# Gate products between the two value halves, the merge's scaled operand transposed first, and a token mix moved into two low-rank factors

## The chip, the cores and the metric

The kernel runs on one core of a Trainium2 chip. A core has five engines with queues of their own: PE (matrix products), DVE (vector), ACT (scalar and activations), POOL (a slower vector engine) and SP (which here only issues loads). Each engine works off its instructions in the order that was fixed when the program was built; engines wait for each other through semaphores. The metric is the device time of one execution in microseconds, the median of several runs.

## What is computed

A block of two models in one program, for 256 tokens of width 1024, all in float32. The part that the change touches is the first layer, an RWKV-7 time mix, of which these lines matter:

```python
h_prev = jnp.pad(h, ((0, 0), (1, 0), (0, 0)))[:, :-1]
hh = h_prev - h
xr = h + hh * mu[0]; xw = h + hh * mu[1]; xk = h + hh * mu[2]
xv = h + hh * mu[3]; xa = h + hh * mu[4]; xg = h + hh * mu[5]
r = xr @ w_r
w = -jax.nn.softplus(-(w0 + jnp.tanh(xw @ w1) @ w2)) - 0.5
k = xk @ w_k
v = xv @ w_v
a = jax.nn.sigmoid(a0 + (xa @ a1) @ a2)
g = jax.nn.sigmoid(xg @ g1) @ g2
...
def step(state, inp):
    r_t, w_t, k_t, v_t, a_t, b_t = inp
    sa = jnp.einsum('bhvk,bhk->bhv', state, a_t)
    state = state * w_t[:, :, None, :] + sa[..., None] * b_t[:, :, None, :] + v_t[..., None] * k_t[:, :, None, :]
    y_t = jnp.einsum('bhvk,bhk->bhv', state, r_t)
    return state, y_t
```

The scan over tokens is computed in four chunks of 64 tokens. In each chunk a triangular system per head has to be inverted (16 heads x 4 chunks). After this layer come a feed-forward block, a differential attention, another feed-forward block, a second token mixer and a third feed-forward block, which the change does not touch.

## The kernel before

The program is written tile by tile; a list scheduler (`schedule_with_timeline_sim=True`, L1333) then fixes the order on each engine from the dependencies, the free buffers and a timeline of its own. What comes earlier in the text goes first where several instructions are ready. `behind(m)` (L230) ties what is traced inside it behind marked instructions of the same engines.

Loads of 512 KB go through five buffers named raw (`wp("raw", 1024, NRAW)`, L263 on SP's queue, L268 on ACT's). Products of weights and activations are made of three products of a rounded part and a rest (`mm3`, L300): ACT casts the rounded part (hi), DVE or POOL subtracts the rest (lo), L273 to L277. Products of plain float32 operands stand in the trace as two records each. PSUM banks of tag p are two.

The early stage (L442 to L483): `normT` squares each token tile (ACT), adds (DVE), takes the root on POOL (L317, `power`), makes a diagonal matrix (DVE, L340) and transposes with it on PE; `ev_x` copies the result to the tiles xn (x0). `mix(j, dst)` (L445) makes one of the six token mixes: a scaled copy on ACT (L452) and a multiply-add with the tokens shifted by one on DVE (L453), 8 each for an unsplit mix. `proj_r(0)` is the first half of the r projection. Then mix 1 and mix 4 (xw, xa) are made, PE multiplies them with the two low-rank factors in wa1 (L471 to L474, 64 columns each) into lat (L475, L476: Tanh and a copy on ACT), then mix 2 (xk), `proj_r(1)`, mixes 5 and 3. Everything after xk waits in ACT's order.

A loop over four feature pairs (L549) makes k, the decays, and the matrices of the chunks (tiles G, MA, MK, RB, BT); its last PE instruction is marked `looped`.

The solve (L647 to L657): DVE transposes the small blocks (tA) and runs 30 elimination steps of two instructions. Meanwhile PE makes the values, `value_proj(n)` for the two halves n of the value width (L512, 16 products of 512 columns each, two banks), and ACT copies them to vt and, per chunk, to uvs (L667). The gate products (L671 to L678) follow in the text: 16 products in four banks of tag p, each emptied by ACT into gl. After the solve DVE makes two transposes, TX (L682) and T0 (L683), and scales T0 (L684). T0 and MA are the operands of the merge's first step (`st == 0`, L698), whose result is copied into V1 (L708); the second step (L701) uses V1 and TT, the latter copied from TX by ACT and DVE (L689). `gate_bias` (L724) multiplies vt by the bonus on DVE (L727). The chunk loop (L736) begins with the products W and then U.

Of the kernel before, what the change touches and what calls it, by code (L numbers as in the profile page):

```python
# [166 lines left out]
def body(ctx, tc, a, at):  # L167
# [26 lines left out]
    def bank(tag, pool=pt, bufs=2):  # L194
        return pool(tag, 512, bufs)
# [22 lines left out]
    def mark(*names):  # L218

        own = {getattr(mybir.EngineType, n) for n in names or ("Pool", "Activation", "DVE")}  # L220
        m = {}
        for i in reversed(nc.cur_bb.bb.instructions):
            if i.engine in own and i.engine not in m:
                m[i.engine] = i
                if len(m) == len(own):
                    break
        return m

    @contextmanager
    def behind(m):  # L230
        with ExitStack() as es:
            for i in m.values():
                es.enter_context(tc.issue_after(i))
            yield
# [4 lines left out]
    def bc(ap, shape):  # L239
        return ap.to_broadcast(shape)  # L240

    def hs(ap, d):
        return ap.rearrange("p (h d) -> p h d", d=d)
# [10 lines left out]
    def C(n):  # L254
        o, w = at[n]
        return cst[:, o:o + w]
# [10 lines left out]
    def wside(name, n=1024, rows=P):  # L267
        t_ = wp("raw", 1024, NRAW)  # L268
        nc.scalar.dma_start(t_[:rows, :n], a[name])
        return t_[:, :n]  # L270
# [26 lines left out]
    def mm(out, l, r, start=True, stop=True):  # L297
        PE.matmul(out, lhsT=l, rhs=r, start=start, stop=stop, skip_group_check=True)  # L298
# [132 lines left out]
    V.tensor_tensor(out=mab[:, 0], in0=g6, in1=mab[:, 1], op=ALU.subtract)  # L431
    xv, rT = FMt(SP, "xv"), [None] * 4
    xr, xk = pairHL(XR, "xr"), pairHL(LP, "xk")
    xw, xa, xg = FMt(EP, "xw"), FMt(EP, "xa"), FMt(XR, "xg")
    x0 = [EP("xn", 4 * (T + 1), 2).rearrange("p (k c) -> p k c", k=4) for _ in range(2)]
    for z in x0:
        G.memset(z[:, :, 0:1], 0.0)
# [7 lines left out]
    def mix(j, dst):  # L445
        for b in range(2):
            for k in (0, 2):
                k2 = slice(k, k + 2)
                d_ = dst.v[b][:, k2] if isinstance(dst, FMt) else hs(scratch("gr", 512, 2), T)
                for f in range(2):  # L450
                    ca, cb = (mab[:, i, j, 4 * b + k + f:4 * b + k + f + 1] for i in range(2))
                    S.activation(d_[:, f], x0[b][:, k + f, 1:], AF.Copy, scale=ca)  # L452
                    V.scalar_tensor_tensor(out=d_[:, f], in0=x0[b][:, k + f, :T], scalar=cb, in1=d_[:, f],  # L453
                                           op0=ALU.mult, op1=ALU.add)
                if not isinstance(dst, FMt):
                    split(d_, dst[0].v[b][:, k2], dst[1].v[b][:, k2], G if j else V)

    def proj_r(i):
        rT[i] = LP("r", 512, 4)
        S.copy(rT[i], pfm(a["w_r"], i, xr, lambda f: None if i else G))  # L460

    mix(0, xr)
    m0 = mark()
    proj_r(0)
    with behind(m0):
        mix(1, xw)
        mix(4, xa)
        m1 = mark()
    lat = LP("lat", 256)
    ps = bank("p")  # L470
    for k in range(8):  # L471
        mm(ps[0:64, :T], wa1[:, k, 0:64], xw.k(k), k == 0, k == 7)
    for k in range(8):
        mm(ps[64:128, :T], wa1[:, k, 64:128], xa.k(k), k == 0, k == 7)  # L474
    S.activation(lat[0:64], ps[0:64, :T], AF.Tanh)  # L475
    S.copy(lat[64:128], ps[64:128, :T])  # L476
    with behind(m1):
        mix(2, xk)
        m2 = mark()
    proj_r(1)  # L480
# [31 lines left out]
    def value_proj(n, acc):  # L512
        for g in range(4):
            w = hs(fetch(a["w_v"], 4 * n + g), 512)
            for k in range(2):
                kk = 2 * g + k
                for t in range(2):
                    with behind(looped):
                        mm(acc[t], xv.k(kk)[:, t * P:(t + 1) * P], w[:, k], kk == 0, kk == 7)
        for t in range(2):  # L520
            S.copy(vt[t][:, n * 512:(n + 1) * 512], acc[t])
# [135 lines left out]
        V.tensor_tensor(out=Tb[:, s + 1:, 0:s], in0=Tb[:, s + 1:, 0:s], in1=tmp[:, s + 1:, 0:s], op=ALU.add)  # L657
    solved = mark("DVE")


    for n in range(2):
        value_proj(n, [bank("v", tps) for _ in range(2)])
    for t in range(2):
        v4 = vt[t].rearrange("p (f h v) -> p f h v", f=8, h=2)
        for c in range(2):
            for hp in range(2):
                S.copy(uvs[2 * t + c][H[1 - hp], :, hp], v4[H[c], :, hp])  # L667
    gl, b1 = FMt(VP, "gl"), FMt(VP, "b1")
    g2a, g2b = wside("lora_g2"), wside("lora_g2b", 1024, 32)
    lnw, lnb = C("lnx_w"), C("lnx_b")  # L670
    for i in range(4):  # L671
        ps = bank("p")
        for f in range(2):
            fb = 2 * i + f
            fs = slice(fb * P, (fb + 1) * P)
            mm(ps[:, F[f]], g2a[:, fs], sgT[:, 0], True, False)
            mm(ps[:, F[f]], g2b[0:32, fs], sgT[0:32, 1], False, True)
        S.copy(gl.v[i // 2][:, 2 * (i % 2):2 * (i % 2) + 2], hs(ps, T))  # L678

    with behind(solved):  # L680
        T0, TX, V1 = hs(tI, 32), tmp, hs(tA, 32)
        V.transpose(TX, Tb)  # L682
        V.transpose(T0, Tb.rearrange("p t s -> p s t"))  # L683
        V.tensor_tensor(out=T0, in0=T0, in1=bc(nsb.rearrange("p f c -> p (f c)").unsqueeze(1), [P, 32, 32]),  # L684
                        op=ALU.mult)
    for qd in (1, 3, 0, 2):
# [651 lines left out]
```

## Time and profile before

| | us |
|---|---|
| median of three runs | 1212.76 (1209.64 to 1217.07) |
| the profiled execution | 1209.02 |
| its span in the trace | 1206.9 |
| PE busy | 1113.0 (92% of the span) |
| DVE busy | 858.0 (71%) |
| ACT busy | 632.5 (52%) |
| POOL busy | 194.4 (16%) |

Times in rows are microseconds from the start of the span of the profiled execution. PE is TensorE's products, PEld its weight loads, which overlap them. The span covers all stages one after another, and the change touches those between 0 and 190 us. A busy PE is not PE at its peak: the granted clock has two levels, 1.00 (2.4 GHz) and 0.50 (1.2 GHz), and the same products take twice the time at the lower one. A chain of waits is followed back from the last instruction: each piece is what released the next one.

### The profile page before, as it was taken

The numbers are of one execution on the slowest core, as the hardware profiler recorded it, in microseconds if no ns is written. First come the engines' busy times: TensorE is split into PE (matmuls) and PEld (weight loads), VectorE is DVE, ScalarE is ACT, GpSimd is POOL, SyncE is SP. The second block draws the span as 40 slices with busy tenths as digits, with TensorE's granted clock in tenths as the row PEclk, the third lists the DMA queues.
The fourth block names the chain that finished last, engine by engine and source line by source line (L and its number), as shares of the span: only waits on it lengthen the run. The fifth ranks groups of instructions, "written<-read, shape, count | busy, mean of one in ns | idle before, by whom it ended". The sixth has DMA issues, their size and how long they took to land.

```text
span 1206.9 us, 19872 instructions
## 1 busy us (share of the span) xinstructions
PE 1113.0 (92%) x7788; PEld 975.2 (81%) x7788; DVE 858.0 (71%) x1508; ACT 632.5 (52%) x1042; POOL 194.4 (16%) x156
## 2 busy tenths in 40 slices
PE   4999999779999999998999999999898789999995
PEld 4788549669999998886679999998876669999994
DVE  5687756859997566856659887554667667877787
ACT  6976145445434346757658334444867446344451
POOL 2242301200000001243130000004001112232320
PEclk8989878889999999999999999999989899999998
DMA  5354220248888563544147997662667234555551
GB/s 191 129 133 129 71 62 32 88 146 278 291 271 310 193 210 103 182 158 139 35 158 261 343 329 251 186 209 81 200 183 195 53 122 138 183 185 188 179 158 53
DMA packets 56589, 205.40 MB, mean 170 GB/s; under 512 B 6288, under 2 KB 6800, under 8 KB 56496
## 3 DMA queue, kind: packets, MB, share of 16 engines
q1 hardware_dynamic: 52128, 189.82, 47.0%
q0 software_dynamic: 2016, 7.34, 3.5%
q10 hardware_dynamic: 2352, 6.98, 1.7%
q8 instruction: 61, 1.00, 0.3%
q14 instruction: 32, 0.26, 0.1%
HBM read 203.06 MB, written 1.05 MB: 169 GB/s over the span
## 4 chain that ended last, share of the span: by engine, by line
PE 74%; DVE 12%; ACT 6%; DMA 5%; issue 2%; POOL 1%; POOLq 0%; ACTq 0%; DVEq 0%
PE p L298 31%; PE tr L298 16%; PE acc L298 14%; PE pj L298 6%; PE sc L298 3%; DVE lo L273 1%; DMA raw<-in_dn 1%; PE W L298 1%; ACT hi L276 1%; PE tr L310 1%; PE G L298 1%; PE px L298 1%; DVE cacc L1304 1%; DVE lo L655 1%; DVE lo L657 1%
## 5 line engine op out<-in xcount | busy, mean ns | idle before, releaser
L276 ACT CAST hi<-raw 128x1024 fp32r<-128x1024 f32 x198 | 205.9, 1047 | 153.9 <-PE p L298 84.1
L273 DVE TENSOR_TENSOR lo<-raw,hi 128x1024 fp32r<-128x1024 f32 x162 | 201.9, 1251 | 83.1 <-ACT hi L276 82.9
L298 PE MATMUL p<-fhh,hi 128*128 128x256 f32 x576 | 164.5, 286 | 2.5 <-ACT fhh L276 1.7
L298 PE MATMUL p<-fhl,hi 128*128 128x256 f32 x576 | 165.0, 286 | 1.2 <-DVE fhl L362 0.9
L298 PE MATMUL p<-fhh,lo 128*128 128x256 f32 x576 | 163.9, 285 | 0.0
L276 ACT CAST dhi<-raw 128x1024 fp32r<-128x1024 f32 x66 | 69.2, 1049 | 133.0 <-DMA raw<-in_dn 133.0
L298 PE MATMUL tr<-fhh,hi 128*128 128x256 f32 x480 | 136.0, 284 | 0.0
L298 PE MATMUL tr<-fhl,hi 128*128 128x256 f32 x480 | 135.9, 283 | 0.0
L298 PE MATMUL tr<-fhh,lo 128*128 128x256 f32 x480 | 135.7, 283 | 0.0
L273 DVE TENSOR_TENSOR dlo<-raw,dhi 128x1024 fp32r<-128x1024 f32 x66 | 83.6, 1267 | 56.7 <-ACT dhi L276 56.7
L273 POOL TENSOR_TENSOR lo<-raw,hi 128x1024 fp32r<-128x1024 f32 x36 | 87.8, 2441 | 189.4 <-ACT hi L276 186.0
L298 PEld LDWEIGHTS p<-fhh,hi 128*128 128x128 f32 x576 | 111.4, 193 | 4.5 <-ACT fhh L276 1.9
L298 PEld LDWEIGHTS p<-fhl,hi 128*128 128x128 f32 x576 | 111.3, 193 | 3.5 <-DVE fhl L362 1.7
L298 PEld LDWEIGHTS p<-fhh,lo 128*128 128x128 f32 x576 | 111.3, 193 | 0.3 <-issue 0.2
L298 PE MATMUL acc<-dhi,acth 128*128 128x512 f32 x264 | 103.6, 392 | 1.3 <-DVE acth L833 1.3
L298 PE MATMUL acc<-dlo,acth 128*128 128x512 f32 x264 | 103.4, 392 | 0.0
L298 PE MATMUL acc<-dhi,actl 128*128 128x512 f32 x264 | 100.7, 390 | 1.0 <-DVE actl L273 1.0
L317 POOL TENSOR_TENSOR s_rstd<-s_ms,mhalf 128x1 f32<-128x1 f32 (+2 forms) x32 | 34.8, 1091 | 361.5 <-DVE s_ms L331 272.4
L298 PEld LDWEIGHTS tr<-fhh,hi 128*128 128x128 f32 x480 | 91.9, 192 | 1.2 <-issue 0.2
L298 PEld LDWEIGHTS tr<-fhl,hi 128*128 128x128 f32 x480 | 91.9, 192 | 1.2 <-issue 0.2
L298 PEld LDWEIGHTS tr<-fhh,lo 128*128 128x128 f32 x480 | 91.9, 192 | 0.0
L888 DVE CUSTOM_DVE_ANT_0 junk<-wada,crow 128x1024 f32<-128x1024 f32 x64 | 78.0, 1219 | 8.9 <-DMA wada<-in_w_ada 7.3
(452 smaller groups left out, 2518.5 us busy)
## 6 DMA issues: line engine op xcount, KB each, us to landing
raw<-in_gu SPq DMA_DIRECT2D x132, 512.0 KB, 4.4
raw<-in_dn SPq DMA_DIRECT2D x66, 512.0 KB, 4.4
wada<-in_w_ada SPq DMA_DIRECT2D x48, 512.0 KB, 5.1
raw<-in_w_r SPq DMA_DIRECT2D x8, 512.0 KB, 4.4
raw<-in_w_k SPq DMA_DIRECT2D x8, 512.0 KB, 3.8
raw<-in_w_v SPq DMA_DIRECT2D x8, 512.0 KB, 4.7
raw<-in_w_o SPq DMA_DIRECT2D x8, 512.0 KB, 4.5
raw<-in_w_ak SPq DMA_DIRECT2D x8, 512.0 KB, 4.4
```

What stands on the lines that cost most here:

```text
L273: (eng or V).tensor_tensor(out=out, in0=raw, in1=hi.bitcast(F32), op=ALU.subtract)
L276: S.copy(hi, raw)
L298: PE.matmul(out, lhsT=l, rhs=r, start=start, stop=stop, skip_group_check=True)
L310: PE.transpose(o, s_, ident)
L317: G.tensor_tensor(out=r, in0=ms, in1=mhalf[:, :n], op=ALU.pow)
L655: V.tensor_tensor(out=tmp[:, s + 1:, 0:s], in0=bc(Ab[:, s + 1:, s:s + 1], shp), in1=bc(Tb[:, s:s + 1, 0:s], shp), op=ALU.mult)
L657: V.tensor_tensor(out=Tb[:, s + 1:, 0:s], in0=Tb[:, s + 1:, 0:s], in1=tmp[:, s + 1:, 0:s], op=ALU.add)
L888: V.tensor_tensor_reduce(out=junk, in0=raw, in1=src, scale=1.0, scalar=0.0, op0=ALU.mult, op1=ALU.add, accum_out=dst[:, e:e + 1])
L1304: V.scalar_tensor_tensor(out=a4[:, ro, co], in0=g4[:, ri, ci], scalar=taps[:, fb, k:k + 1], in1=a4[:, ro, co], op0=ALU.mult, op1=ALU.add)
```

## The change

Three edits, all in the first layer.

1. The mixes xw and xa are no longer made. Since a mix is a x_t + b x_(t-1) with a and b per feature, a and b are multiplied into the two low-rank factors instead: four products on POOL (`G.tensor_tensor`, 128 partitions x 8 x 64 each) make wmix[0] and wmix[1], each with the 64 columns of both factors. PE then multiplies wmix[0] with x0 and wmix[1] with x0 shifted by a token, 16 products of 128 columns into one bank. They stand, with Tanh and copy, ahead of mix 0 and `proj_r(0)` in the text. Mix 2 is now tied behind mix 0 instead of mix 4. The pool EP holds two tiles of wmix in place of four of xw and xa.
2. The gate products become a function that is called between `value_proj(0)` and `value_proj(1)`. The output tiles gl and b1 and the loads of the gate weights (`wside`, on ACT's queue) are now ahead of both value halves in the text, and the copies to uvs come after them.
3. T0 is transposed before TX.

```diff
--- before.py
+++ after.py
@@ -431,7 +431,13 @@
     V.tensor_tensor(out=mab[:, 0], in0=g6, in1=mab[:, 1], op=ALU.subtract)
     xv, rT = FMt(SP, "xv"), [None] * 4
     xr, xk = pairHL(XR, "xr"), pairHL(LP, "xk")
-    xw, xa, xg = FMt(EP, "xw"), FMt(EP, "xa"), FMt(XR, "xg")
+    xg = FMt(XR, "xg")
+
+    wmix = [hs(EP("wmix", 1024, 2), P) for _ in range(2)]
+    for i in range(2):
+        for j, c in ((1, slice(0, 64)), (4, slice(64, P))):
+            G.tensor_tensor(out=wmix[i][:, :, c], in0=wa1[:, :, c], in1=bc(mab[:, i, j].unsqueeze(2), [P, 8, 64]),
+                            op=ALU.mult)
     x0 = [EP("xn", 4 * (T + 1), 2).rearrange("p (k c) -> p k c", k=4) for _ in range(2)]
     for z in x0:
         G.memset(z[:, :, 0:1], 0.0)
@@ -459,22 +465,17 @@
         rT[i] = LP("r", 512, 4)
         S.copy(rT[i], pfm(a["w_r"], i, xr, lambda f: None if i else G))
 
+    lat = LP("lat", 256)
+    ps = bank("p")
+    for k in range(8):
+        for i in range(2):
+            mm(ps[:, :T], wmix[i][:, k], x0[k // 4][:, k % 4, 1 - i:1 - i + T], k + i == 0, k + i == 8)
+    S.activation(lat[0:64], ps[0:64, :T], AF.Tanh)
+    S.copy(lat[64:128], ps[64:128, :T])
     mix(0, xr)
     m0 = mark()
     proj_r(0)
     with behind(m0):
-        mix(1, xw)
-        mix(4, xa)
-        m1 = mark()
-    lat = LP("lat", 256)
-    ps = bank("p")
-    for k in range(8):
-        mm(ps[0:64, :T], wa1[:, k, 0:64], xw.k(k), k == 0, k == 7)
-    for k in range(8):
-        mm(ps[64:128, :T], wa1[:, k, 64:128], xa.k(k), k == 0, k == 7)
-    S.activation(lat[0:64], ps[0:64, :T], AF.Tanh)
-    S.copy(lat[64:128], ps[64:128, :T])
-    with behind(m1):
         mix(2, xk)
         m2 = mark()
     proj_r(1)
@@ -657,30 +658,33 @@
         V.tensor_tensor(out=Tb[:, s + 1:, 0:s], in0=Tb[:, s + 1:, 0:s], in1=tmp[:, s + 1:, 0:s], op=ALU.add)
     solved = mark("DVE")
 
-
-    for n in range(2):
-        value_proj(n, [bank("v", tps) for _ in range(2)])
+    gl, b1 = FMt(VP, "gl"), FMt(VP, "b1")
+    g2a, g2b = wside("lora_g2"), wside("lora_g2b", 1024, 32)
+    lnw, lnb = C("lnx_w"), C("lnx_b")
+
+    def gate_products():
+        for i in range(4):
+            ps = bank("p")
+            for f in range(2):
+                fb = 2 * i + f
+                fs = slice(fb * P, (fb + 1) * P)
+                mm(ps[:, F[f]], g2a[:, fs], sgT[:, 0], True, False)
+                mm(ps[:, F[f]], g2b[0:32, fs], sgT[0:32, 1], False, True)
+            S.copy(gl.v[i // 2][:, 2 * (i % 2):2 * (i % 2) + 2], hs(ps, T))
+
+
+    value_proj(0, [bank("v", tps) for _ in range(2)])
+    gate_products()
+    value_proj(1, [bank("v", tps) for _ in range(2)])
     for t in range(2):
         v4 = vt[t].rearrange("p (f h v) -> p f h v", f=8, h=2)
         for c in range(2):
             for hp in range(2):
                 S.copy(uvs[2 * t + c][H[1 - hp], :, hp], v4[H[c], :, hp])
-    gl, b1 = FMt(VP, "gl"), FMt(VP, "b1")
-    g2a, g2b = wside("lora_g2"), wside("lora_g2b", 1024, 32)
-    lnw, lnb = C("lnx_w"), C("lnx_b")
-    for i in range(4):
-        ps = bank("p")
-        for f in range(2):
-            fb = 2 * i + f
-            fs = slice(fb * P, (fb + 1) * P)
-            mm(ps[:, F[f]], g2a[:, fs], sgT[:, 0], True, False)
-            mm(ps[:, F[f]], g2b[0:32, fs], sgT[0:32, 1], False, True)
-        S.copy(gl.v[i // 2][:, 2 * (i % 2):2 * (i % 2) + 2], hs(ps, T))
-
     with behind(solved):
         T0, TX, V1 = hs(tI, 32), tmp, hs(tA, 32)
+        V.transpose(T0, Tb.rearrange("p t s -> p s t"))
         V.transpose(TX, Tb)
-        V.transpose(T0, Tb.rearrange("p t s -> p s t"))
         V.tensor_tensor(out=T0, in0=T0, in1=bc(nsb.rearrange("p f c -> p (f c)").unsqueeze(1), [P, 32, 32]),
                         op=ALU.mult)
     for qd in (1, 3, 0, 2):
```

## Rows read from the trace of the kernel before

**Rows 1.** The chain that ended last, over the whole span, in order of time: start us, length us, engine, tile and line, count.
```profile
298.75 5.75 PE p L298 x48
```

**Rows 2.** The same chain, read for 120 to 250 us (a name ahead of the tile's own, as lo or tI, is the buffer's first name).
```profile
160.58 0.11 DVE lo L657
160.72 1.25 DVE lo L682
161.96 1.83 DVE tI L683
...
166.24 1.24 DVE tI L684
...
167.61 3.00 PE mg L298 x100
170.62 4.60 PE p L298 x8
175.22 0.58 PE mg L298 x16
175.79 4.60 PE p L298 x8
180.39 3.87 PE mg L298 x140
184.26 5.68 PE W L298 x32
189.94 1.89 PE p L298 x16
```

**Rows 3.** The timeline of all engines, 132 to 168 us: start us, us from the first start to the last end, engine, line, operation, out<-in, shapes, count (of PE two records for one product of float32); in brackets the idle time before it and what ended that.
```profile
132.54 27.82 PE L298 MATMUL v<-raw,xv 128*128 128x512 f32 x64
...
160.20 4.59 PE L298 MATMUL p<-sgT,raw 128*128 128x256 f32 x16
```

**Rows 4.** Busy time of PE alone in stretches of 2 us (records begun), then its granted clock, the DMA share and GB/s.
```profile
164.00:166.00 2.00, 0.79 (x3) 1.00 0.04 14
...
168.00:170.00 2.00, 2.00 (x79) 0.50 0.03 8
...
188.00:190.00 2.00, 2.00 (x17) 0.94 0.00 0
```

**Rows 5.** The timeline of ACT, 160 to 200 us.
```profile
162.05 4.29 ACT L689 COPY TT<-lo 32x512 f32<-32x512 f32 x4 [5.35 <-DVE lo L682]
...
166.99 2.50 ACT L667 COPY uv<-vt 64x512 f32<-64x512 f32 x4
169.39 1.05 ACT L678 COPY gl<-p 128x512 f32<-128x512 f32 x2
```

**Rows 6.** The timeline of DVE, 160 to 200 us.
```profile
169.52 1.23 DVE L727 TENSOR_TENSOR vt<-vt,bonus 128x1024 f32<-128x1024 f32 x1 [2.05 <-ACT uv L667]
170.78 0.68 DVE L708 COPY tA<-mg 32x512 f32<-32x512 f32 x1
```

**Rows 7.** Busy time of all engines in one stretch, in the order PE, PEld, DVE, ACT, POOL, then the granted clock, the DMA share and GB/s.
```profile
37.00:63.00 26.00, 21.00 (x166) 19.19 (x165) 17.57 (x29) 25.18 (x47) 8.04 (x9) 0.98 0.52 162
```

**Rows 8.** The timeline of all engines, 0 to 70 us.
```profile
15.75 0.69 DVE L440 COPY xn<-tr 128x512 f32<-128x512 f32 x1 [1.41 <-PE tr L298]
...
19.09 2.53 DVE L273 TENSOR_TENSOR lo<-raw,hi 128x1024 fp32r<-128x1024 f32 x1 [1.08 <-ACT hi L276]
...
25.05 3.30 ACT L452 ACTIVATE xw<-xn,mab 128x256 f32<-128x256 f32 x8
...
25.78 3.25 DVE L453 SCALAR_TENSOR_TENSOR xw<-xn,mab,xw 128x256 f32<-128x256 f32 x8
...
28.25 3.30 ACT L452 ACTIVATE xa<-xn,mab 128x256 f32<-128x256 f32 x8
...
30.76 3.02 PE L298 MATMUL p<-xw,raw 128*64 128x256 f32 x13
...
34.94 0.57 ACT L460 COPY r<-p 128x512 f32<-128x512 f32 x1
...
37.01 0.39 PE L298 MATMUL p<-xrh,hi 128*128 128x256 f32 x1
```

**Rows 9.** The timeline of POOL, 0 to 140 us.
```profile
11.37 0.55 POOL L317 TENSOR_TENSOR s_rstd<-s_ms,mhalf 128x1 f32<-128x1 f32 x1 [1.91 <-DVE s_ms L331]
...
18.19 2.35 POOL L273 TENSOR_TENSOR lo<-raw,hi 128x1024 fp32r<-128x1024 f32 x1 [2.29 <-ACT hi L276]
...
126.13 1.90 POOL L622 TENSOR_TENSOR bkw<-BK,wc 128x1024 f32<-128x1024 f32 x1 [3.58 <-DVE BK L579]
```

**Rows 10.** The instructions that write or read the tile raw, issued in the first 1.4 us: the load of the first lora factor by ACT's queue (start 1.2 us), and the time from its issue to its landing.
```profile
L269 ACTq DMA_DIRECT2D raw<-in_lora x1: 452/452/452, 1.2 to 1.2; - x1
...
DMA to landing us min/median/max: 8.8/8.8/8.8
```

**Rows 11.** The timeline of PE, 60 to 135 us.
```profile
83.56 7.29 PE L298 MATMUL p<-xg,raw 128*128 128x256 f32 x32
```

**Rows 12.** The timeline of PE, 106 to 134 us.
```profile
119.86 0.38 PE L298 MATMUL tr<-cst,sqk 128*128 128x2 f32 x2 [1.22 <-ACT sqk L568]
123.38 0.66 PE L298 MATMUL G<-PR,BK 64*64 64x128 f32 x2 [3.13 <-DVE BK L581]
```

**Rows 13.** The page's sixth part, DMA issues: out<-in, queue, count, KB each, median us from issue to landing.
```profile
raw<-in_w_v SPq DMA_DIRECT2D x8, 512.0 KB, 4.7
```

## The prediction

> **What bounds the kernel now.** I read the chain that ended last first: most of it is PE, in long blocks like the 48 products that take 5.75 us, 0.12 each [rows 1]. So a change pays where PE waits, where it works at the lower clock, or where work leaves it. Then I read the chain around the three edits, the timelines of the engines named there, and PE's granted clock in short stretches.
>
> In the merge, the chain shows [rows 2]: the solve on DVE ends at 160.69, then two transposes, then the scaling of the operand at 166.24, and only then the 32x32 products of the merge at 167.61. They do not run through: two gate blocks of 4.60 us each stand among them, and the state loop's first products (tile W) start at 184.26. The timeline shows why [rows 3, 5]: PE ran both value halves from 132.54 to 160.36 without a break and the first half of the gate products by 164.79; the other half waited for the two banks of tag p, which ACT emptied only at 169.39, after its TT copies (4.29 us) and uv copies. The clock table [rows 4] adds the price: full clock at 164 to 166, half (1.2 GHz) from 168 to about 188. Eight gate records take 4.60 us there [rows 2]; sixteen took 4.59 us at full clock [rows 3]. So 9.20 us of the merge stage are gate products at half clock.
>
> In the early stage, PE runs the two low-rank products between two projections, from 30.76 to 37.01 [rows 8]. Their inputs cost ACT 3.30 + 3.30 us from 25.05 to 31.5, and DVE about as much beside it [rows 8]. Right after, ACT is busy 25.18 of 26 us while PE idles 5 [rows 7]: ACT's order bounds 37 to 63. Whatever leaves ACT before 37 comes off the time, as far as nothing else is late.
>
> **Gate products between the value halves.** The 64 value records take 27.82 us [rows 3], a half 13.8. So half 0 ends at 146.3; the gate products, now one block, cost 2 x 4.59 = 9.2 us at full clock, to 155.5; half 1 ends at 169.3. ACT has nothing longer than a bank copy there, so the p banks turn. The merge can begin at 169.3 instead of 167.61: 1.7 us later. Against that, 9.20 us leave the merge. The products that remain take 3.00 + 0.58 + 3.87 = 7.45 us [rows 2].
>
> What is late next is the copy of the first merge step. On DVE the bonus product of the second token tile stands ahead of it and waits for ACT's uv copies [rows 6]. I keep this order: half 1 ends 169.3, the value copy takes about 0.6, the uv copies 2.50 [rows 5] (to 172.4), the bonus product 1.23 (173.6), then DVE copies both halves at 0.68 [rows 6] (175.0) and ACT its part of the second, at the gl rate of rows 5 about 0.6 (175.6). The second half of step two, 64 records at 3.00/100 us [rows 2], ends at 177.5. W then starts at 177.5 instead of 184.26: **6.8 us** gained. Bounds: if W's products fill PE's wait before the copies, only U (189.94 now) waits for the merge; it could start at 177.5 + 0.68 + 0.6 = 178.8, a gain of 11.1. I don't take that: in the trace PE stood idle from 164.79 to 167.61 and W did not move in. From below: each us by which half 1 ends late costs one; I allow 4 (one landing of a value chunk is 4.7 [rows 13]), a gain of 2.8. The two gate weights, loaded over ACT's queue, now come ahead of the value chunks and hold two of the five load buffers; with three left, a chunk is used every 27.82/8 = 3.5 us, three in 10.4, against 4.7 + 3.5, so no stall.
>
> **Operand transposed first.** After the solve the order becomes T0 (1.83), TX (1.25), scaling (1.24) [rows 2]: ready at 165.0 instead of 167.48. That is worth nothing here, for half 1 holds PE until 169.3. That cover is 4.3 us; if the gate products moved out of this stage, the full 2.5 us would count.
>
> **Mix moved into the factors.** Removed: 16 ACT and 16 DVE instructions [rows 8] and 6.25 us of PE between the projections. Added on PE: 16 products with 128 columns and 256 moving; the same form, 32 records, took 7.29 us [rows 11]. (The Trainium skill, page "TensorE: Matmul & The Clock Gate", section "LDWEIGHTS (loading the stationary operand)", says that the weight load grows with its columns, P/1.2 ns; 64 more in 32 records would be 1.7 us as an estimate. The rows give 7.29 - 6.25 = 1.0, and I use the rows.) They now stand ahead of the first projection. The first factor's load buffer is free some 20 us earlier, which removes no stall that I see.
>
> Added on POOL: four products of 512 columns with a broadcast operand. A broadcast product of 1024 took 1.90 [rows 9], so 0.95 each from below, and half of a 2.35 us split, 1.18, from above; I take 1.05, as the broadcast row is the nearest: 4.2 in all. They can start when the lora factor lands, 1.2 + 8.8 = 10.0 [rows 10], so they end at 14.2. The root of the second token tile runs at 11.37 [rows 9] on the same queue, and its x lands later than that, so I expect the four products ahead of it: the root moves to 14.2, 2.8 us late, and with it the last xn copy, from 16.44 [rows 8] to 19.2. The low-rank products then run from about 18.5, the first 3 or 4 records at twice the 0.228 us of rows 11 because PE was idle before, to 26.5; the projection's 48 products at 0.12 us [rows 1] end at 32.3. So the next projection starts at 32.3 instead of 37.01: PE gains 4.7. ACT is free for the next mix at 25.05, 6.4 us earlier, but it then meets the copy of that projection's result, at 34.94 before [rows 8]. I take **4.5 us**. Bounds: 6.4 if the root is not delayed; 0 if ACT stands at the copy or the Tanh until PE's gain is gone.
>
> A row that speaks against POOL: DVE's split took 2.53 us at 19.09 [rows 8] beside POOL's at 18.19 [rows 9]; DVE alone needs about 1.2 for that size. (The Trainium skill, page "GPSIMD Engine Reference", section "8. Key points", says that POOL shares its SBUF interfaces with VectorE; the trace agrees. By it, POOL's two splits, pushed behind the products into DVE's first mix, would cost DVE up to 1.3 each, and the early gain would be about 3.2.) The sum leaves this out, because DVE waits on ACT in that mix as well.
>
> **Sum.** 6.8 + 4.5 = 11.3 us. The profiled execution took 1209.02 (span 1206.9), so 1197.7 there; it lies 3.7 below the median of the runs shown, and in their terms 1212.76 - 11.3 = 1201.4: I forecast **1201**.
>
> **The rivals.**
> 1. *The gate products slip into the loop's tail.* Nothing ties them behind the loop, and their weights now come ahead of the value chunks. PE idles 1.22 and 3.13 us there [rows 12]. Then the merge begins when the scaled operand is ready, 165.0, so 4.3 us more are gained: 15.6 in all, 1197. For it: idle PE, free p banks. Against it: their output tile takes memory of the loop's tiles.
> 2. *The early gain is lost.* ACT, in order, waits for the Tanh or the copy and the stage keeps its length: 6.8 are left, 1206. For it: the second root behind four POOL products. Against it: ACT's 6.6 us are gone for certain.
> 3. *The change does little.* Both moves are given back, for instance if DVE's order puts the bonus products before the merge and the roots are late: within 3 us of 1212.8.
> 4. *Slower: the load ring runs dry.* If only one buffer is left to the value chunks, each of seven waits out its landing of 4.7 [rows 13]: 33 us late, minus 11.3, about 1234. With two buffers it costs about 1.3 per pair, 4 in all, so it decides from one buffer down.
>
> **How the numbers follow.** The measurement tells about 1% from no change, 12 us. Forecast 0.45, with its own range 1197 to 1206 (the POOL price and the late copy); rival 1 0.25; rival 2 0.17; rival 3 0.08; rival 4 0.05. A gain over 12 us: 0.4 of the forecast (the root not delayed, or W earlier) and nearly all of rival 1, 0.18 + 0.23 = 0.41. Slower by over 1%: rival 4, 0.05. The rest, 0.54, is within 1%. The range drops rival 4 and the outer half of rival 3 and takes the bound of W's filling: 1190 to 1210.
>
> **What would show it.** In the profile after: value records in two blocks with the gate records between, all at full clock; no gate record among the merge's; scaling before the TT copies on DVE; W near 173 (all times 4.5 earlier by the early gain); four POOL products between 10 and 15 with the second root behind them; low-rank products before the first projection, and the next projection near 32. I am wrong if half 1 ends later than about 165 in the new trace, if gate records stand before the loop's last products, or if PE still starts the second projection at 36 or later.

## The result

The kernel after took 1196.98 us in the median of four runs (1194.1 to 1200.62), the kernel before 1211.2 beside it: ratio 0.9883, 95% interval 0.9853 to 0.9913, that is 14.2 us less (10.5 to 17.8). A second series of six runs of the same kernel gave 0.9907 (0.9876 to 0.9937), 11.3 us (7.6 to 15.0). The forecast was 11.3 us less, 1201. The profiled execution took 1198.87, its span 1197.1.

The chain that ended last, 105 to 200 us, in the kernel after; it answers to [rows 2]:

```profile
111.75 6.42 PE p L298 x28
...
128.27 10.50 PE v L298 x24
138.77 2.94 PE p L298 x10
141.71 3.43 PE v L298 x8
145.14 1.88 PE p L298 x6
147.01 13.93 PE v L298 x32
160.95 3.75 PE mg L298 x128
...
165.44 0.59 ACT tA L712
...
168.57 1.23 DVE vt L731
169.80 0.60 DVE TT L714
...
170.48 0.58 ACT TT L714
...
171.11 4.57 PE W L298 x24
175.67 1.89 PE p L298 x16
```

No gate block of 4.60 us stands in the merge any more: 128 merge records start at 160.95, right behind the last value product. The 32 gate records that [rows 2, 3] show at 160 and inside the merge stand before and inside the value products: of the 28 records from 111.75, 16 are gates, and 10 + 6 stand at 138.77 and 145.14. The chunk loop's U products (p, x16) start at 175.67 instead of 189.94, 14.3 earlier. The piece of DVE and ACT between 165.44 and 171.11 is the place that the prediction called the late copy, one merge step later than it was put.

PE's timeline of the kernel after, the gate records in the loop's gap; [rows 12] show the two waits that they fill:

```profile
113.19 4.98 PE L298 MATMUL p<-sgT,raw 128*128 128x256 f32 x16
```

PE's granted clock in the kernel after, in the columns of [rows 4]:

```profile
162.00:164.00 2.00, 2.00 (x80) 1.00 0.70 236
...
168.00:170.00 2.00, 2.00 (x37) 0.50 0.00 0
...
176.00:178.00 2.00, 2.00 (x29) 1.00 0.00 0
```

The clock still falls inside the merge (1.00 at 162, 0.50 at 168), but what runs at the half level now are merge and W products, no gates, and it is back by 176 instead of about 188 [rows 4].

DVE's timeline of the kernel after, against [rows 6]:

```profile
156.29 1.19 DVE L688 TENSOR_TENSOR tI<-tI,nsb 128x1024 f32<-128x1024 f32 x1
...
162.91 0.68 DVE L712 COPY tA<-mg 32x512 f32<-32x512 f32 x1 [2.94 <-PE mg L298]
...
168.57 1.23 DVE L731 TENSOR_TENSOR vt<-vt,bonus 128x1024 f32<-128x1024 f32 x1 [0.73 <-ACT uv L683]
169.72 0.67 DVE L714 COPY TT<-mg 32x512 f32<-32x512 f32 x1
```

The operand is scaled from 156.29 to 157.48, 3.4 before PE takes it. The first merge copies (L712) wait for PE alone. Behind them a bonus product (L731) waits for ACT's uv copies and holds back the last TT copy.

The early stage, timeline of all engines of the kernel after, against [rows 8, 9]:

```profile
9.35 0.29 DVE L340 TENSOR_SCALAR dg<-cst,s_rstd 128x128 f32<-128x128 f32 x1 [0.55 <-POOL s_rstd L317]
...
9.91 4.04 POOL L439 TENSOR_TENSOR wmix<-raw,mab 128x512 f32<-128x512 f32 x4 [0.60 <-DMA raw<-in_lora]
...
13.91 0.55 POOL L317 TENSOR_TENSOR s_rstd<-s_ms,mhalf 128x1 f32<-128x1 f32 x1
...
14.43 4.66 POOL L273 TENSOR_TENSOR lo<-raw,hi 128x1024 fp32r<-128x1024 f32 x2
14.49 2.36 DVE L340 TENSOR_SCALAR dg<-cst,s_rstd 128x128 f32<-128x128 f32 x1 [0.29 <-POOL s_rstd L317]
...
16.77 3.39 DVE L273 TENSOR_TENSOR lo<-raw,hi 128x1024 fp32r<-128x1024 f32 x1
...
16.95 3.24 PE L298 MATMUL tr<-dg,xres 128*128 128x128 f32 x16 [3.48 <-issue]
...
19.99 7.55 PE L298 MATMUL p<-xn,wmix 128*128 128x256 f32 x32
...
27.18 0.47 PE L298 MATMUL p<-xrh,hi 128*128 128x256 f32 x1
```

Four factor products take 4.04, and the second root goes from 11.37 to 13.91, both as forecast. Beside POOL's splits (14.43 to 19.09) DVE's 128-column scaling dg takes 2.36, where the first token tile's took 0.29, and its split 3.39. The low-rank products follow at 19.99, the first projection at 27.18, the second at 33.12.

Busy time of all engines, columns of [rows 7]:

```profile
37.00:63.00 26.00, 23.45 (x189) 21.08 (x189) 21.50 (x39) 24.97 (x45) 7.48 (x6) 0.91 0.52 147
```

ACT is still nearly full from 37 to 63 (24.97 of 26), and PE's idle time has gone from 5.0 to 2.55 us, at a granted clock of 0.91 where it was 0.98.

### The profile page after: what moved, and what is told of

Its sections match the earlier page's. It is cut to its first block, busy times and chain, and to the rows that moved or that the text cites. A ratio compares the mean times of both kernels' runs of the same rounds, so it can differ in the third digit from the quotient of the medians.

```text
span 1197.1 us, 19840 instructions
## 1 busy us (share of the span) xinstructions
PE 1112.6 (93%) x7788; PEld 975.6 (81%) x7788; DVE 853.7 (71%) x1492; ACT 625.3 (52%) x1026; POOL 196.4 (16%) x160
## 3 DMA queue, kind: packets, MB, share of 16 engines
HBM read 203.06 MB, written 1.05 MB: 171 GB/s over the span
## 4 chain that ended last, share of the span: by engine, by line
PE 74%; DVE 10%; ACT 6%; DMA 5%; issue 3%; POOL 1%; SPq 0%; POOLq 0%; ACTq 0%; DVEq 0%
PE p L298 31%; PE tr L298 14%; PE acc L298 13%; PE pj L298 6%; PE sc L298 3%; PE v L298 2%; DMA raw<-in_dn 2%; DVE cacc L1308 2%; DVE lo L273 1%; ACT hi L276 1%; PE W L298 1%; PE tr L310 1%; PE px L298 1%; DMA raw<-in_w_r 1%; PE G L298 1%
```

## The experiments

The instructions behind the first layer stand in the same order in both kernels, so places before that are the finest measure: the last pair's k copy (end of the early gain), the merge's first product, U's first product, and Y's first root on POOL (all in us from the span's start). Ratios are to the kernel before, with 95% intervals; where only one execution was timed, its time stands, and the kernel before took 1206.81 beside it.

| kernel | k copy | merge | U | root of Y | time |
|---|---|---|---|---|---|
| before | 118.68 | 167.61 | 189.87 | 213.31 | 1 |
| after | 113.39 | 160.88 | 175.60 | 199.04 | 0.9883 (0.9853 to 0.9913) |
| e9_after_again | 114.49 | 163.50 | 177.79 | 201.23 | 0.9907 (0.9876 to 0.9937) |
| e1_mix_only | 114.76 | 163.66 | 185.86 | 209.30 | 0.9988 (0.9967 to 1.0009) |
| e2_gates_only | 119.12 | 165.06 | 181.42 | 205.06 | 0.9947 (0.9926 to 0.9968) |
| e3_t0_only | 118.16 | 164.44 | 189.37 | 212.81 | 0.9996 (0.9969 to 1.0022) |
| e4_after_tx_first | 113.67 | 161.15 | 175.88 | 199.33 | 1203.51 |
| e5_gates_tied | 114.40 | 166.84 | 182.49 | 206.03 | 0.9968 (0.9946 to 0.9991) |
| e6_no_gates | 113.21 | 160.49 | 175.77 | 199.20 | 1195.69 |
| e7_roots_first | 115.33 | 164.34 | 180.61 | 204.05 | 1201.55 |
| e8_no_lora | 112.49 | 158.37 | 172.44 | 195.87 | 1191.86 |
| e10_uv_late | 117.47 | 163.40 | 177.35 | 200.79 | 0.9895 (0.9860 to 0.9931) |
| e11_root_between | 112.52 | 160.00 | 174.70 | 198.14 | 0.9889 (0.9844 to 0.9934) |
| e12_between_late | 112.42 | 159.90 | 174.29 | 197.73 | 0.9909 (0.9875 to 0.9944) |

The k copy differs between executions. Up to it the seven traces after, e9, e1, e4, e5, e6 and e10 have the same order of instructions, and it comes at 113.2 to 117.5, 114.5 on average; the three traces before, e2 and e3 have the other order, and it comes at 118.2 to 119.1, 118.7 on average. So single k copies that differ by a microsecond or two say little, and later places are best read from the k copy.

**One edit alone.** Edit 1 on the kernel before is the first and second hunk of the diff, edit 2 the gate function and its call (in the third), edit 3 this:

```diff
-        V.transpose(TX, Tb)
         V.transpose(T0, Tb.rearrange("p t s -> p s t"))
+        V.transpose(TX, Tb)
```

> The kernel before with edit 1 alone (mix moved into the factors). Theory (the three edits add up, and this one is the early gain): the k copy of the last pair at about 113.4 instead of 118.68, the merge's first product about 5 to 6 earlier than 167.61 (162 to 163), the root of Y at 207 to 208 instead of 213.31; by the times about 1206, 5.3 below the kernel before. Rival (the early gain is real only because the gate products fill the loop's tail, or it is given back in the middle because the value chunks or the solve do not follow): the k copy is early, but the root of Y is less than 3 earlier.

> The kernel before with edit 2 alone (gate products between the value halves; TX still transposed first, mixes still made). Theory (16 gate records go into the loop's gap also here, and the gate products are nearly the whole of the middle gain): 10 to 16 gate records before the first value record, the merge's first product at 165 to 166.5, bound by the scaled operand rather than by PE, W's products at 176 to 178, the root of Y 8 to 9 earlier than 213.31, that is 204 to 205; by the times about 1203. Rival (the order of the transposes is needed for the gain): the merge waits 2 or more for its operand and the root of Y is less than 6.5 earlier.

> The kernel before with edit 3 alone (T0 transposed before TX). Theory (worth nothing, or a loss, while the gate products still hold PE: the scaled operand comes about 1.2 to 2.5 earlier, but ACT's TT copies start about 1.9 later, and with them the gl copies on which the two half-clock gate blocks wait): the first merge product at 165 to 166.4, W no earlier than 183.5, the root of Y between 212 and 215.3. Rival (the operand is what bounds the merge by itself): the root of Y 2.0 to 2.5 earlier, 210.8 to 211.3.

Edit 1: the k copy of the third pair comes at 97.81 instead of 103.28, 5.5 earlier, that of the last 3.9 earlier, because the clock fell for one stretch at 109 (0.54 and 0.61 between 108.8 and 112.8). From there on the 3.9 is carried to the root of Y (4.0). That is less than the 5.3 expected, and the times give only 1.5 us, with 4.0 as the end of the interval; so the early gain is shown at its places in the trace, but by its own times not to its full size. Edit 2: 16 gate records at 118.93 in the loop's gap and the root of Y 8.25 earlier, as the theory said; but the merge (165.06) follows the last value product, with its operand ready at 164.55, so PE bounds it and not the operand, as the theory had it. Edit 3: the merge starts 3.2 earlier, but then both gate blocks stand together at half clock (16 records, 9.27 us from 171.10); measured from the k copy, the root of Y moves by 0.02. At the root of Y the three add up to 4.0 + 8.25 + 0.5 = 12.8, between the 14.3 and 12.1 of the two profiles of the kernel after. By the times they add up to 1.5 + 6.4 + 0.5 = 8.4, below the 14.2 and 11.3 of the kernel after; with these intervals the sum of the times is neither confirmed nor refuted.

**T0 first, inside the kernel after.** The same two lines the other way round.

> The kernel after with TX transposed before T0 again; the fixed order of DVE differs from that of the kernel after in these four instructions alone. Theory (as predicted: with the gate products out of the merge PE holds the merge back, so the order of the transposes is worth nothing): the scaled operand is ready 2.4 later, at about 159.9, still before the merge's first product at 160.9; the root of Y within 0.7 of 199.04. Rival (the operand bounds the merge since half of the gate products slipped into the loop's gap): merge and root of Y 1.5 to 2.5 later, 200.5 to 201.5.

The operand is ready at 160.37, the merge starts at 161.15, and from the k copy to the root of Y it is 85.66 against 85.65. Worth nothing, as predicted; but with TX first only 0.8 us of cover is left, where the prediction's numbers give 1.8 (169.3 - 167.48).

**Gates kept out of the loop's gap.**

```diff
-                mm(ps[:, F[f]], g2a[:, fs], sgT[:, 0], True, False)
-                mm(ps[:, F[f]], g2b[0:32, fs], sgT[0:32, 1], False, True)
+                with behind(looped):
+                    mm(ps[:, F[f]], g2a[:, fs], sgT[:, 0], True, False)
+                    mm(ps[:, F[f]], g2b[0:32, fs], sgT[0:32, 1], False, True)
```

> The kernel after with the gate products tied behind the loop's last PE instruction, so that none can go into the loop's gap. Theory (the 16 records in the gap are what put the time below the forecast's sum): the 16 records return behind the loop, 5 us later ending value half 1, the merge's first product at about 165 to 166 instead of 160.88, W at 175 to 176.5, the root of Y at 203 to 204.5 instead of 199.04; by the times about 4 to 5 above the kernel after, 1201 to 1202. Rival (PE in the loop's gap was not free, or the loop's end clock was warmer only because of them, or the operand at 157.5 has spare time enough): the root of Y less than 2.5 later.

PE's timeline of this kernel:

```profile
127.33 1.61 PE L298 MATMUL p<-sgT,raw 128*128 128x256 f32 x4
...
130.40 3.83 PE L298 MATMUL p<-sgT,raw 128*128 128x256 f32 x12
```

The 16 records return behind the loop (1.61 + 3.83). Against the second profile of the kernel after, whose k copy comes at nearly the same time (114.49 and 114.40), the merge starts 3.3 later and the root of Y comes 4.8 later: the theory. (Against the first profile, read from the k copy, it is 5.0 and 6.0.) By the times the loss is larger than the 4 to 5 expected: 0.9968 against 0.9883 and 0.9907 is 10.3 and 7.4 us. So the loop's gap is worth more than what the gain has beyond the forecast: without it 7.3 us are left at the root of Y and 3.9 by the times (1.1 to 6.5), less than the 11.3 forecast. What filling it costs can be read from all runs: from the k copy to the first value product it is 13.2 to 16.3, 14.6 on average, in the nine kernels with 16 gate records between (5 us of work), and 13.8 to 14.7, 14.0 on average, in the four without.

**No gate products at all.**

```diff
-            ps = bank("p")
...
-            S.copy(gl.v[i // 2][:, 2 * (i % 2):2 * (i % 2) + 2], hs(ps, T))
+            h2 = slice(2 * (i % 2), 2 * (i % 2) + 2)
+            S.copy(gl.v[i // 2][:, h2], xv.v[i // 2][:, h2])
```

> The kernel after without its gate products: gl is copied by ACT from xv instead, so the output is another. Theory (where they now stand they cost little: those in the loop's gap nothing, those between the values about the 5.05 us that they take, and of that all but about 3.4 is given back because the scaled operand then bounds the merge): value half 1 ends at about 155 to 156, the merge's first product at 157.5 to 159.5, the root of Y 1.5 to 3.5 earlier than 199.04. Rival (all of their 10 us of PE are still on the path): the root of Y 8 to 10 earlier. Third possibility (without them in the loop's gap the clock falls and the loop's tail is longer by what they cost): the root of Y within 1 of 199.04.

PE's timeline of this kernel:

```profile
127.89 27.82 PE L298 MATMUL v<-raw,xv 128*128 128x512 f32 x64
160.49 3.80 PE L298 MATMUL mg<-tI,MA 32*32 32x32 f32 x128 [4.78 <-DVE tI L683]
```

The values end at 155.7, but the merge waits 4.78 us for its operand, and the root of Y is where it was (199.20). Here the gap stood empty, the clock was at 0.50 from 116.5 to 126.5, the solve began 1.8 later (130.64 instead of 128.87), and DVE put a bonus product of 1.19 ahead of the scaling; the third possibility. So taking the gates from where they now stand brings nothing: the operand, 2.8 later by the later solve and the bonus product (159.11 for 156.29), then bounds the stage. What they would cost with the same clock and the same order on DVE is not shown.

**What is left in the early stage.** First the factor products behind both roots, then the low-rank products left out, then the root between the two pairs of factor products.

```diff
-    for i in range(2):
...
+    roots = mark("Pool")
...
+            with behind(roots):
+                G.tensor_tensor(out=wmix[i][:, :, c], in0=wa1[:, :, c], in1=bc(mab[:, i, j].unsqueeze(2), [P, 8, 64]),
+                                op=ALU.mult)
```

```diff
-            mm(ps[:, :T], wmix[i][:, k], x0[k // 4][:, k % 4, 1 - i:1 - i + T], k + i == 0, k + i == 8)
-    S.activation(lat[0:64], ps[0:64, :T], AF.Tanh)
+    S.activation(lat[0:64], wmix[0][0:64, 0:2].rearrange("p k c -> p (k c)"), AF.Tanh)
...
```

```diff
-    for i in range(2):
+    def factor_products(i):
...
-    for t in range(2):
-        normT(xres[t], t, ev_x)
+    normT(xres[0], 0, ev_x)
+    factor_products(0)
+    normT(xres[1], 1, ev_x)
+    roots = mark("Pool")
+    with behind(roots):
+        factor_products(1)
```

> The kernel after with the four factor products moved behind both roots on POOL. Theory (the second root, pushed from 11.4 to 13.91 by the four products, holds back the transposes, the low-rank products and with them the whole early stage): second root at about 11.3, transposes of the second token tile about 2.5 earlier, low-rank products at 17.5 to 18.5 instead of 19.99, second projection at 30.5 to 31.5 instead of 33.0, the k copy of the last pair at 111 to 112 instead of 113.39. Rival (POOL's two splits, pushed from 14.43 to about 16.5, or ACT's order, hold back what follows all the same): the k copy within 0.7 of 113.39.

> The kernel after without the 16 low-rank products on PE: Tanh and copy read the factor tiles instead, so the output is another. Theory (in 20 to 33 us ACT's order and the mix that it makes bound the stage, and PE's 7.55 us of low-rank products are hidden beside them): the first projection starts at 24 to 25 instead of 27.18, the second at 31.5 to 33.0 instead of 33.0, the k copy of the last pair 0 to 1.5 earlier than 113.39. Rival (PE bounds the early stage, so these products are what is left to gain): the second projection at 27 to 29, the k copy 4 to 6 earlier, 107.5 to 109.5.

> The kernel after with the second root on POOL between the two pairs of factor products. Theory (the root's lateness is what is left in the early stage): root at about 12.0 instead of 13.91, the second tile's transposes 1.5 to 2 earlier than 16.95, low-rank products at 17.5 to 18.5, the first k copy 1.5 to 3 earlier than 49.78; and, if ACT's order carries it through, the k copy of the last pair 1 to 2 earlier than 113.39. Rival (as with both roots first: DVE is slowed beside POOL's splits, a weight load or another order of ACT takes the gain back): the k copy of the last pair within 0.7 of 113.39, or later.

Behind both roots: the low-rank products start at 15.15, 4.8 earlier, and the first pair's k copy comes at 46.73 instead of 49.78; but the last pair's comes at 115.33, 1.9 later. Neither theory said that. DVE's timeline, then POOL's, then PE's, of this kernel; last PE's without the low-rank products and of the kernel before:

```profile
15.96 5.74 DVE L461 SCALAR_TENSOR_TENSOR gr<-xn,mab,gr 128x256 f32<-128x256 f32 x4
...
24.02 1.68 DVE L461 SCALAR_TENSOR_TENSOR gr<-xn,mab,gr 128x256 f32<-128x256 f32 x4
```

```profile
15.77 4.86 POOL L273 TENSOR_TENSOR lo<-raw,hi 128x1024 fp32r<-128x1024 f32 x2
```

```profile
57.17 0.39 PE L298 MATMUL p<-xkh,lo 128*128 128x256 f32 x1 [3.38 <-DMA lo<-in_w_k]
```

```profile
56.71 0.39 PE L298 MATMUL p<-xkh,lo 128*128 128x256 f32 x1 [3.38 <-DMA lo<-in_w_k]
```

```profile
62.99 0.58 PE L298 MATMUL p<-xkh,lo 128*128 128x256 f32 x1 [3.24 <-DMA lo<-in_w_k]
```

Four multiply-adds of the first mix take 5.74 us beside POOL's splits and 1.68 after them; later PE waits 3.38 for a weight load (lo<-in_w_k, the second pair's k weights), and ACT loads its tables four times between 58 and 71 us instead of twice. The program's order changed on ACT, DVE and PE with the edit, so how the loss divides among these stays open. The wait for that load is 3.1 to 3.2 in the three traces without edit 1 and at most 0.6 in the seven with the order of the kernel after; the prediction has no such term. Without the low-rank products (7.55 us of PE) the last k copy is only 0.9 earlier, as the theory said; but the first pair's is 4.1 earlier (45.64), and then PE waits 3.38 for the same load. So what bounds the early stage is not shown: it may be ACT's order, as the theory has it, or that load. Its root of Y is 3.2 earlier, of which 1.6 lie between k copy and value products, where the clock differs from run to run. With the root between the pairs (12.10 instead of 13.91) the k copy is 0.9 earlier and so is the root of Y: between theory and rival, and within what executions of one order differ by. The first pair's k copy is 2.4 later (52.23), where the theory had it 1.5 to 3 earlier.

**The merge's end, and both together.**

```diff
-    for t in range(2):
+    def uv_copies(t):
...
+    uv_copies(0)
...
+    merged = mark("DVE", "Activation")
+    with behind(merged):
+        uv_copies(1)
```

> The kernel after, unchanged, beside the three variants that follow: a second profile and more times. Theory (what the trace loses again behind 457 us, where the order of the instructions is the same in both kernels, is the clock of that run and no cost of the change): the root of Y within 0.7 of 199.04, the stages behind it shift otherwise than in the first profile, and the ratio to the kernel before at 0.988 to 0.991. Rival (the change costs 3 to 5 us behind 457 us in every run): the same loss at the same place again, and a ratio nearer 0.993.

> The kernel after with the second token tile's four uv copies (and through them its bonus product) tied behind the merge's last copies; the fixed orders of PE and POOL stay as they are, on ACT and DVE only these instructions change places. Theory (the bonus product and the uv copies ahead of the TT copies hold back W by 0.27 and keep U waiting): the last TT copy on ACT at about 169.5 instead of 170.48, no wait inside W, U 0.3 to 1.0 earlier than 175.60, the root of Y at 198.0 to 198.7; in the times not to be told from the kernel after. Rival (U is bound by W's products alone): the root of Y within 0.3 of 199.04.

> Both of the last two edits on the kernel after, as a version that might beat it. Theory (they add): the root of Y 1.5 to 3 earlier than 199.04, 196 to 197.5, and 2 us by the times. Rival (the early one gives nothing): the root of Y within 1 of 199.04 and the same time as the kernel after.

ACT's timeline with the late uv copies:

```profile
170.28 0.58 ACT L716 COPY TT<-mg 32x512 f32<-32x512 f32 x1 [1.61 <-DVE TT L716]
172.01 0.58 ACT L716 COPY TT<-mg 32x512 f32<-32x512 f32 x1 [1.16 <-DVE TT L716]
172.61 2.50 ACT L683 COPY uv<-vt 64x512 f32<-64x512 f32 x4
```

The uv copies leave the chain and no wait is left inside W, but from the merge's start to U it is 13.95 against 14.29 in the second profile of the kernel after: 0.34 (14.39 against 14.70, 0.31, with the root between the pairs in both). W's 32 records then run for 6.28 without a break. Both edits together bring the root of Y to 197.73, 1.3 earlier than the kernel after, less than the theory's 1.5 to 3, and the times do not tell it from that kernel. So there is no version here that measurably beats it.

The kernel after, measured again, has its root of Y at 201.23, outside the 0.7 expected, since its k copy came 1.1 later and the clock fell inside the gate block in the gap (5.87 instead of 4.98). Further on it went the theory's way. Busy time of all engines in one stretch, first of the first profile, then of the second:

```profile
500.00:617.00 117.00, 108.73 (x504) 83.13 (x503) 66.09 (x132) 69.03 (x170) 36.25 (x22) 0.93 0.36 115
```

```profile
500.00:617.00 117.00, 109.26 (x532) 84.77 (x532) 70.31 (x141) 71.63 (x177) 38.04 (x22) 0.99 0.39 122
```

In the first profile the clock was lower there (0.93 against 0.99), and between two roots on POOL (L331) that lie 130.2 apart in the kernel before (487.06 and 617.26) it took 136.7; in the second, with the same instructions, 130.8. So the first profile's loss behind 457 us is no cost of the change.

## Why the prediction came out as it did

**The sum** (11.3) was right in size: 14.2 and 11.3 by the times, 14.3 and 12.1 at the root of Y. That is in part luck. One of the prediction's own signs of being wrong is met: gate records stand before the loop's last products (113.19 against 127.18). With all gates behind the loop, as the sum has them, e5 gains 7.3 at the root of Y and 3.9 by the times, and its middle gain is 3.1 at U where the sum has 6.8: from merge to U it takes 15.65 where the sum has 13.9, and the 32 gate records take 10.5 where it has 9.2. What the sum had too much came back from the loop's gap, which was rival 1 and not in the sum. By the first series alone, 1197, rival 1's number fits better than the forecast.

**Early gain, 4.5: measured 5.3 and 4.2 at the k copy in the two profiles, 4.2 between the averages of the seven and the three traces.** The first steps held: factor products at 1.01 each against the 1.05 taken, root at 13.91 against 14.2, first projection at 27.2 against 26.5. Two terms were mis-sized and offset each other in part. PE's products took 7.2 to the start of the projection, not 8.0. The cost of POOL's splits to DVE, which the sum left out, came in another place than the prediction's first mix: dg and the split, 2.36 and 3.39, so that the low-rank products start at 19.99 and not 18.5. (The Trainium skill, "GPSIMD Engine Reference", section "8. Key points", has POOL and VectorE share their SBUF interfaces; the 5.74 against 1.68 us in e7 agree.) The size came in part by another road than the sum's: at the second projection the gain is 3.9 and 2.7 in the two profiles (33.12 and 34.26 for 37.01), at the first pair's k copy 2.8 and 1.6, and only behind that 5.3 and 4.2. Between these places the kernel before waits 3.24 for a weight load and the kernel after 0 and 0.3. Why that load no longer holds PE up was not tried.

**Low-rank products with 128 columns.** The 1.0 that the prediction reads from 7.29 - 6.25 is no price of the columns, for 7.29 runs to the end of the last record and 6.25 to the start of the next product. With 64 and with 128 columns alike 11 records begin in 2 us at full clock, and a record lasts 0.38; only the weight loads, which overlap them, are longer (0.19 for 0.14). The instructions on the tile, then busy time of PE, PEld, DVE and ACT on it in 2 us, of the kernel before, then the same of PE, PEld and POOL in e1:

```profile
L298 PEld LDWEIGHTS p<-xw,raw x16: 133/137/137, 30.8 to 33.8; 128*64 128x64 f32 x16
L298 PE MATMUL p<-xw,raw x16: 379/379/430, 30.8 to 34.0; 128*64 128x256 f32 x16
...
31.00:33.00 2.00, 2.00 (x11) 1.26 (x10) 0.00 (x0) 0.00 (x0) 1.00 0.02 4
```

```profile
L298 PEld LDWEIGHTS p<-xn,wmix x32: 188/189/198, 20.2 to 26.8; 128*128 128x128 f32 x32
L298 PE MATMUL p<-xn,wmix x32: 377/378/382, 20.3 to 27.0; 128*128 128x256 f32 x32
...
22.00:24.00 2.00, 2.00 (x11) 1.74 (x10) 0.00 (x0) 1.00 0.94 352
```

From first start to the next product it is 6.25 before, 6.73 in e1 and 7.19 in the kernel after, whose first records run at half clock. (The Trainium skill, "TensorE: Matmul & The Clock Gate", section "LDWEIGHTS (loading the stationary operand)", has the load grow with its columns, P/1.2 ns, which as an estimate is 0.053 us for 64 more. The loads here agree, but PE's time shows nothing of it.)

**Middle gain, 6.8: measured 9.0 and 7.9 (U's gain less the k copy's).** That 9.20 us of half-clock gates leave the merge was right. That all 32 gate records then stand between the values was wrong: rival 1 came true in half. Nothing tied the gates behind the loop, and 16 of them, as many as two p banks hold, went into its gap; e5 prices that at 3.3 for the merge's start and 4.8 at the root of Y against the second profile, and at 5.0 and 6.0 against the first. The prediction's reason against it, that gl takes memory of the loop's tiles, did not keep the products out. The full price of rival 1 was not reached, for the other 16 records still stand among the values; in e6 removing them too brought nothing, because the operand comes later there.

**The late copy.** The step was right in its mechanism and wrong in its place: not the first merge copy stands behind a bonus product that waits for uv, but the last. Merge to U was put at 13.9 (169.3 to 177.5, and 5.7 of W) and measured 14.7 and 14.3. e10, which takes the uv copies away, returns 0.34.

**T0 first, 0:** confirmed alone (e3) and inside the kernel after (e4). Its cover was 3.4 us in place of 4.3: half 1 ended 8.4 earlier than put (160.9 for 169.3), the operand came 7.5 earlier (157.5 for 165.0).

**Rivals 2 to 4.** The early gain was carried through to the root of Y (e1: 3.9 and 4.0), and both series gain more than rival 2 (6.8 us) and rival 3 (at most 3 us) leave. The load ring did not run dry: 32 value records ran in 14.00 us without a break, as in half of [rows 3].

## What to carry to other kernels

Work that is free of a chain goes where the engine idles while it waits for that chain: 16 gate records put into a gap of 4.4 us cost 0.6 on average, in runs that differ by 3, while 16 of them behind a wait at half clock cost 9.2. Ask of every moved group what ties it to its new place; where nothing does, the scheduler may put it earlier still, and that case needs its price. Once a group is hidden, look at what bounds next: here removing it altogether brought nothing. And a total that comes out right does not show that its terms were: measure the arrangement that the sum described, as e5 does.

## What the runs showed of the hardware

The merge's first step does not follow the clock: PE takes 44 of its 32x32 records in a microsecond at full clock in the kernel after and 43 at half clock in e6. The second step does, though by less than two: 61 at full clock in e5, 46 at half in the kernel after. So the sentence ahead of the prediction that the same products take twice the time at the lower level holds for the gate products, but for neither of these. In the code the first step's moving operand, T0, is read with a stride of 32 elements, the second's is contiguous; whether that is the reason was not tried. PE's busy time of the same stretch, two lines of the kernel after, one of e6, one of e5:

```profile
162.00:163.00 1.00, 1.00 (x44) 1.00 0.65 172
...
167.00:168.00 1.00, 1.00 (x46) 0.50 0.00 0
```

```profile
162.00:163.00 1.00, 1.00 (x43) 0.50 0.08 16
```

```profile
170.00:171.00 1.00, 1.00 (x61) 1.00 0.01 4
```

Unbroken work just before did not keep the clock up here: in the kernel after PE ran without a break from 109.4 to 119.4 at full clock, and the clock was at 0.63 in the two microseconds after that and at 0.50 from 121.4, among transposes with two moving columns and 64x64 products.

```profile
117.40:119.40 2.00, 2.00 (x13) 1.00 0.00 0
119.40:121.40 2.00, 2.00 (x16) 0.63 0.00 0
121.40:123.40 2.00, 2.00 (x28) 0.50 0.02 4
```
